# One float32 kernel of two transformer blocks: in the second block's mixers the group-norm transposes later, weight splits held back, pooled tiles in another order, and the norm factors spread one tile of k later

## The chip, the cores and the metric

The kernel runs on one core of one Trainium2 chip. The metric is the device time of one execution in microseconds (us). Engines are called PE (TensorE, matrix multiply), DVE (VectorE), ACT (ScalarE), POOL (GpSimd) and SP (the queue that issues most transfers).

## What is computed

The reference runs two transformer blocks one after the other on 256 tokens of width 1024, all in float32. Most edits lie in the second block; its core:

```python
for i in range(DEPTH):                       # DEPTH = 2
    mod = (cond @ ada_w[i] + ada_b[i]).reshape(bn, 3, 3, D_MODEL)
    h = modulate(rms_norm(x, ffn_norm[i, 0]), mod[:, 0, 0], mod[:, 0, 1])
    x = x + 0.5 * mod[:, 0, 2][:, None, :] * swiglu(h, w_gate[i, 0], w_up[i, 0], w_down[i, 0])
    h = modulate(rms_norm(x, mix_norm[i]), mod[:, 1, 0], mod[:, 1, 1])
    if i % 2 == 0:   # 31-tap conv, group_layer_norm (8 groups), silu | short gated conv
        y = conv_mixers(h, conv_w_in, ..., conv_w_out)
    else:            # means over trailing windows 2, 4, 8, 16, each a 128x128 linear | MoBA attention
        y = pool_moba_mixers(h, pm_w_in, pool_w, ..., pm_w_out)
    x = x + mod[:, 1, 2][:, None, :] * y
    h = modulate(rms_norm(x, ffn_norm[i, 1]), mod[:, 2, 0], mod[:, 2, 1])
    x = x + 0.5 * mod[:, 2, 2][:, None, :] * swiglu(h, w_gate[i, 1], w_up[i, 1], w_down[i, 1])
return rms_norm(x, final_norm)
```

The first block (four attention branches and a convolutional feed-forward, also twice) has the same shape of stages: a norm, a wide product, elementwise work, a product back to width 1024, a residual.

## The kernel before

**Layout.** Activations lie transposed: 1024 features are 8 tiles k of 128 partitions, tokens run along the free axis (272 with the 16 meta tokens in the first block, 256 in the second). An output tile is 128 features by all tokens in one PSUM bank.

**Three products for one.** Each float32 operand is split into a high and a low part (fp32r), `x = xh + xl`, and `mm3` issues three matmuls for each k: high by high, low by high, high by low. For a weight of 128x1024, `split` (line 114) writes `wh` on ACT and `split_low` (line 122) writes `wl = raw - wh` on DVE. So a weight costs PE 24 matmuls for each output tile, ACT one activation and DVE one subtraction.

**The weight stream.** All weights are one stream of chunks in order of use. `pump_dma` loads them on SP into three `raw` buffers, `prefetch` splits as far ahead as there are buffers (three of the pool `wp`, and five spare ones in the second block), `get` hands the next one to PE and asks for more. Where a split is issued on ACT and DVE is set only by where `get` or `prefetch` is called in the program: each engine works through its instructions in program order.

**Pipes and the side generator.** An output tile's eviction is a generator in steps; `advance` takes the next step of each after the next tile's matmuls, `drain` finishes all. Work of another kind (the conv taps and group norm, `gen_conv`; the attention, `gen_att`) is a side generator, of which `tick` issues a step or a few after a PE item.

**Products back into the residual.** In a mixer, `gated_gemm` is called with an order of two halves of k, (4, 0) for the conv mixer and (0, 4) for the pool mixer. A pass makes all 8 output tiles from four of the eight k, with 12 matmuls each; line 1824 adds the tile, times its gate, to the residual `h`. In the second pass `evict` also makes the square (line 1831), the raw high part `uh` (322) and the raw low part `ul` (326) of the next stage's input, and the sum of squares on POOL (1849).

**Norm after the product.** The next stage's first product, `first_gemm`, does not wait for the norm: it multiplies the raw `uh`, `ul` (gain applied, norm factor not) by four weights at once, k by k (12 matmuls a k in the second block, 9 in the first block's groups of three). After k = 1 it sums the squares over features by matmuls with ones (`tok_sums`), DVE and POOL make the factor `rs`, and after a later k `spread` copies it to all partitions by matmuls with `ident`; ACT puts the result into `pr` (line 367). Then `normed` writes the finished `uh`, `ul` for the products that follow (16 DVE operations of lines 302 and 297, 8 ACT ones of line 306, each able to overwrite a k only after PE has read it), the four output tiles are multiplied by `pr` (385), get their shift (388, 389), and `prefetch(2)` splits two weights. There are nine such products: four in the first block, five in the second.

**Group norm in the conv mixer.** `norm(j0)` runs as steps of the side generator, for channel tiles 2, 3 and then for 0, 1: mean, squares, variance, `gnr` on POOL, two transposes on PE (line 2080), `ind` matmuls that spread the factor, two products on DVE (2092), Silu on ACT (2096), the split into `oh` and `ol` (237, 238). The second pass of the product back begins with channel tile 0.

**Pooling.** `ev_u` evicts a tile u of 128 channels (line 2283), doubles its window by adds on DVE (2288: one add for window 2, four for 16), scales it and subtracts (2293, 2294). `mixed` then multiplies the four results by 128x128 weights `pw` and splits them, as input of the first pass of the product back.

Of the kernel before, what the change touches and what calls it, by code (L numbers as in the profile page):

```python
# [62 lines left out]
class Kern:  # L63
    def __init__(self, tc, a, out, w):

        self.tc, self.nc, self.a, self.out, self.w = tc, tc and tc.nc, a, out, w
        self.items = []
        self.side = deque()
        self.pipes = deque()
        self.rate = 1  # L70
        self.wait = 0
        self.spare, self.n_phase = 0, 0
        self.h = self.uh = self.ul = self.acc = self.norm = None


# [53 lines left out]
    def prefetch(self, n=99, ahead=99):  # L129

        self.pump_dma()
        while self.n_split < min(len(self.subq), self.n_used + ahead) and n:
            n -= 1
            c, _ = self.subq[self.n_split]
            out = [x for k, x in self.where.items() if self.held or k >= self.n_used]
            spare = c.spare > 0 and c.spare == self.phase and sum(out) < self.n_spare
            if not spare and len(out) - sum(out) >= NS:  # L140
                break
            while c.tile is None and self.lows:
                self.split_low()
            if c.tile is None:
                break
            self.split(self.n_split, spare)
            self.where[self.n_split] = spare
            self.n_split += 1
# [190 lines left out]
    def first_gemm(self, mk, evict, groups):  # L339

        nc = self.nc
        raw = self.norm is not None
        gain, shift, c, sums = self.norm or (None, None, slice(0, T), None)
        self.norm = None
        n, c0 = c.stop - c.start, 2 if shift else 0
        first = 0  # L350
        for g, size in enumerate(groups):
            tiles = [(w, *ms[0]) for w, ms in zip(self.get(size), mk[first:])]
            pss = [(self.gps if i < 3 else self.aps)() for i in range(size)]
            self.held = size > 1
            for k in range(KD):
                for (w, m0, m1), ps in zip(tiles, pss):
                    self.mm3(
                        ps[: m1 - m0, : n + c0], w, k, m0, m1, (self.uh, self.ul), k, c.start - c0, n + c0,
                        k == 0, k == KD - 1,
                    )  # L360
                if raw and g == 0 and k == 1:
                    r, bl = sums()
                elif raw and g == 0 and k == 2:
                    ps = self.spread(r, bl)
                    o = c.start if bl[-1][0] > 128 else 0
                    pr = self.wk.tile([128, T], F32, tag="pr", name="pr", bufs=1)[:, :n]
                    nc.scalar.activation(pr, ps[:, o : o + n], AF.Copy)
                elif k in (4, 6):
                    self.prefetch(1)
                    self.advance()  # L370
                yield
            self.held = False
            if not raw:
                for i, ps in enumerate(pss):
                    self.prefetch(1)
                    self.advance()
                    self.pipe(evict(first + i, ps))
                first += size
                continue
            if g == len(groups) - 1:  # L380
                self.normed(self.h[:, :, c], pr, gain, shift, n, (self.uh[:, :, c], self.ul[:, :, c]))
            ts = []
            for ps, (w, m0, m1) in zip(pss, tiles):
                t, m = self.w1(n), m1 - m0
                nc.vector.tensor_tensor(out=t[:m], in0=ps[:m, c0 : c0 + n], in1=pr[:m], op=MUL)
                if shift:
                    b = self.sm.tile([128, 1], F32, tag="fb", name="fb", bufs=2)
                    nc.vector.tensor_copy(b[:m], ps[:m, 0:1])
                    nc.scalar.activation(t[:m], t[:m], AF.Identity, bias=b[:m])
                ts.append(t)  # L390
            self.prefetch(2)
            while self.lows:
                self.split_low()
            for i, t in enumerate(ts):
                self.pipe(evict(first + i, t))
            first += size
            yield
# [1409 lines left out]
    def gated_gemm(self, w, kt, x, i, s, half, nxt, order=None, between=None):  # L1807
# [45 lines left out]
        for n, k0 in enumerate(order or ()):  # L1853
            end = n == len(order) - 1
            if end and between:
                between()
            for j0 in (0, 4):
                def fn(j0=j0, k0=k0, end=end):
                    if j0 == 0:
                        self.drain()  # L1860
                    xx = x()
                    for q in range(2):
                        (wt,) = self.get()
                        for m in range(2):
                            ps = self.gps()
                            for kk in range(4):
                                self.mm3(
                                    ps[:, :SEQ], wt, kk, 128 * m, 128 * m + 128, xx, k0 + kk, 0, SEQ, kk == 0, kk == 3
                                )
                            self.advance()  # L1870
                            self.pipe(evict(j0 + 2 * q + m, ps, end))
                            yield

                rows = w[k0 * 128 : k0 * 128 + 512, j0 * 128 : j0 * 128 + 512]
                self.add(fn, Chunk(rows, [[(0, 0, 256)], [(256, 0, 256)]]))
# [73 lines left out]
    def conv_mixer(self):  # L1949
# [102 lines left out]
        def norm(j0):  # L2052
# [20 lines left out]
            nc.vector.tensor_scalar(out=ms, in0=pv[:, 0:8], scalar1=1.0 / 64, scalar2=EPS, op0=MUL, op1=ADD)  # L2073
            r = self.sm.tile([128, 8], F32, tag="gn", name="gnr", bufs=2)
            nc.gpsimd.tensor_tensor(out=r, in0=ms, in1=self.mhalf[:, :8], op=ALU.pow)
            for _ in range(2 if j0 == 0 else 1):
                yield
            ps = self.aps()
            for b in range(2):
# [9 lines left out]
            for q in range(2):  # L2089
                j = j0 + q  # L2090
# [93 lines left out]
    def pool_mixer(self):  # L2184
# [123 lines left out]
        self.add(start)  # L2308
        for j in (0, 2):
            cols(1536 + 128 * j, to("v", j))  # L2310
        for j in (0, 2):
            cols(128 * j, ev_u(j))

        def mixed():
            for g in range(4):
                ps = self.gps()
                self.mm(ps[:, :SEQ], S["pw"][:, g, :], S["p", g])
                t = S["u"][:, g, 16:]
                nc.scalar.activation(
                    t, ps[:, :SEQ], AF.Identity, scale=self.v("pool_scale_2", g), bias=S["pb"][:, g : g + 1]  # L2320
                )
                self.split_act(S["oh"][:, g, :], S["ol"][:, g, :], t)
            yield

        self.add(mixed)
        self.gated_gemm(
            self.w["pm_w_out_2"][0], KD, lambda: (S["oh"], S["ol"]), 1, 1, False, (1, 2, "ffn_norm_2", 3), (0, 4),
            lambda: self.add(lambda: self.finish(G["g"])),
# [175 lines left out]
```

## Time and profile before

| | |
|---|---|
| runs | median 2204.09 us of 3 (2201.56 to 2204.61) |
| profiled execution | 2204.02 us, its span 2202.0 us |
| PE busy | 2137.4 us, 97% of the span |
| DVE busy | 1597.9 us, 73% |
| ACT busy | 1195.7 us, 54% |
| POOL busy | 173.4 us, 8% |
| granted PE clock, mean | 0.992 of full speed |
| transfers | 443.42 MB, mean 201 GB/s |

In a timeline row the first number is the start in us from the span's start, the second how long the instruction (or the merged run of `x` instructions) took; in brackets stands the engine's idle time ahead of it and whose end released it. PE's matmuls overlap: in an unbroken row of them one of 0.28 us starts every 0.12 us, so a bracket on PE leaves out some 0.16 us of the delay of the next start. In a row of waits stand the engine that waited, for whom, the us in total, how many times and the longest. In a row of the table by stretches stand the stretch, its length, each engine's busy us and instructions, the granted PE clock as a share of 2.4 GHz, the DMA share and GB/s.

### The profile page before, as it was taken

Reading aid. Unit: us, or ns where it says so; the run is one execution under the profiler, and the core shown is the slowest. Engines: PE = TensorE matmul, PEld = TensorE weight load, DVE = VectorE, ACT = ScalarE, POOL = GpSimd, SP = SyncE. Lnnn points to the kernel's source line nnn. Section 1 sums busy time; section 2 is a strip of 40 time slices with the busy share of each in tenths; the row PEclk is TensorE's granted clock in tenths of the full one; section 3 lists DMA queues with packets and bytes.
Section 4 is the critical chain, followed back from the end, with each engine's and each line's share of the span. In section 5 each row is a group of like instructions: output and inputs, shape, how many; then the busy total and the mean of one; then the engine's idle time right before and its main releaser. Section 6 shows DMA issues by size and latency. Waiting matters only on the chain. (4 is left out here: it accounts for less than half of the span.)

```text
span 2202.0 us, 42228 instructions
## 1 busy us (share of the span) xinstructions
PE 2137.4 (97%) x17234; PEld 2051.9 (93%) x17234; DVE 1597.9 (73%) x2833; ACT 1195.7 (54%) x2164; POOL 173.4 (8%) x223
## 2 busy tenths in 40 slices
PE   7999999999989999999999899999999999999998
PEld 7898989899979899898999899999999999989998
DVE  5665555888985656558989877797877877777553
ACT  4556454667456554547765644455544544476442
POOL 1320111100031101111000100001000000001000
PEclk9999999999999999999999999999999999999999
DMA  7653234454854342345559687555777687744552
GB/s 281 196 199 125 97 134 156 180 181 174 316 201 161 126 151 104 128 167 184 207 186 361 240 289 270 216 204 189 253 276 285 253 284 269 261 154 163 183 178 72
DMA packets 74322, 443.42 MB, mean 201 GB/s; under 512 B 14477, under 2 KB 15821, under 8 KB 26128
## 3 DMA queue, kind: packets, MB, share of 16 engines
q1 hardware_dynamic: 63312, 423.85, 53.7%
q0 software_dynamic: 10528, 16.79, 2.6%
q8 instruction: 135, 2.21, 0.4%
q14 instruction: 59, 0.48, 0.1%
q10 hardware_dynamic: 288, 0.07, 0.0%
HBM read 437.32 MB, written 10.01 MB: 203 GB/s over the span
## 5 line engine op out<-in xcount | busy, mean ns | idle before, releaser
L227 PE MATMUL g<-uh,wh 128*128 128x256 f32 (+2 forms) x3560 | 1028.0, 289 | 11.1 <-ACT uh L322 6.2
L227 PE MATMUL g<-ul,wh 128*128 128x256 f32 (+2 forms) x3560 | 1019.9, 286 | 10.8 <-DVE ul L326 6.3
L227 PE MATMUL g<-uh,wl 128*128 128x256 f32 (+2 forms) x3560 | 1016.6, 286 | 3.2 <-DVE wl L122 3.2
L122 DVE TENSOR_TENSOR wl<-raw,wh 128x1024 fp32r<-128x1024 f32 (+2 forms) x668 | 787.9, 1185 | 274.5 <-ACT wh L114 273.2
L114 ACT ACTIVATE wh<-raw 128x1024 fp32r<-128x1024 f32 (+2 forms) x668 | 678.3, 1020 | 348.3 <-PE g L227 313.7
L227 PEld LDWEIGHTS g<-uh,wh 128*128 128x128 f32 x3560 | 674.3, 189 | 34.1 <-issue 13.8
L227 PEld LDWEIGHTS g<-ul,wh 128*128 128x128 f32 x3560 | 673.1, 189 | 16.4 <-DVE ul L326 7.1
L227 PEld LDWEIGHTS g<-uh,wl 128*128 128x128 f32 x3560 | 675.1, 190 | 4.4 <-DVE wl L122 4.0
L227 PE MATMUL g<-gh,wh 128*128 128x256 f32 (+1 forms) x1056 | 299.2, 283 | 0.0
L227 PE MATMUL g<-gh,wl 128*128 128x256 f32 (+1 forms) x1056 | 299.2, 283 | 0.0
L227 PE MATMUL g<-gl,wh 128*128 128x256 f32 (+1 forms) x1056 | 299.0, 283 | 0.0
L227 PEld LDWEIGHTS g<-gl,wh 128*128 128x128 f32 x1056 | 201.5, 191 | 0.0
L227 PEld LDWEIGHTS g<-gh,wh 128*128 128x128 f32 x1056 | 201.3, 191 | 0.0
L227 PEld LDWEIGHTS g<-gh,wl 128*128 128x128 f32 x1056 | 201.3, 191 | 0.0
L1774 DVE CUSTOM_DVE_ANT_0 adaw<-adaw,condb,vec 128x1024 f32<-128x1024 f32 x144 | 182.4, 1279 | 0.0
L1677 DVE SCALAR_TENSOR_TENSOR y<-edge,vec,y 128x272 f32<-128x272 f32 (+1 forms) x176 | 86.4, 493 | 29.5 <-ACT y L1672 26.2
L227 PE MATMUL g<-oh,wh 128*128 128x272 f32 (+1 forms) x296 | 87.8, 297 | 0.0
L227 PE MATMUL g<-ol,wh 128*128 128x272 f32 (+1 forms) x296 | 84.8, 287 | 0.0
L227 PE MATMUL g<-oh,wl 128*128 128x272 f32 (+1 forms) x296 | 84.8, 286 | 0.0
L1920 ACT ACTIVATE sg<-g 128x256 f32<-128x256 f32 x80 | 30.5, 382 | 99.1 <-PE g L227 99.0
L1276 ACT ACTIVATE gt<-g 128x272 f32<-128x272 f32 (+1 forms) x64 | 25.1, 392 | 101.8 <-PE g L227 101.7
L1670 ACT ACTIVATE edge<-g 128x272 f32<-128x272 f32 (+1 forms) x82 | 32.3, 393 | 59.3 <-PE g L227 59.1
(384 smaller groups left out, 2311.5 us busy)
## 6 DMA issues: line engine op xcount, KB each, us to landing
raw<-in_weights_dram SPq DMA_DIRECT2D x298, 1024.0 KB, 5.0
adaw<-in_ada_t_dram SPq DMA_DIRECT2D x72, 1024.0 KB, 6.1
raw<-in_weights_dram SPq DMA_DIRECT2D x28, 768.0 KB, 5.0
skew<-scr POOLq DMA_DIRECT2D x6, 1086.0 KB, 23.0
h<-skew POOLq DMA_DIRECT2D x16, 272.0 KB, 3.7
h<-skew POOLq DMA_DIRECT2D x8, 512.0 KB, 5.2
condb<-cond SPq DMA_DIRECT2D x5, 512.0 KB, 4.7
hd<-h SPq DMA_DIRECT2D x2, 1088.0 KB, 8.9
```

The costliest lines, as they stand in the source:

```text
L114: self.nc.scalar.activation(h3[:, :, d0 : d0 + n], c.tile[:, :, c0 : c0 + n], AF.Copy)
L122: self.nc.vector.tensor_tensor(out=l3[:, :, d0 : d0 + n], in0=c.tile[:, :, c0 : c0 + n], in1=h3[:, :, d0 : d0 + n].bitcast(F32), op=SUB,)
L227: self.nc.tensor.matmul(out, lhsT, rhs, start=start, stop=stop, skip_group_check=True)
L1276: nc.scalar.activation(t[:, :rn], ps[:, :rn], AF.Tanh, scale=0.5)
L1670: nc.scalar.activation(e[:, 1 + r0 : 1 + r0 + rn], ps[:, :rn], AF.Copy)
L1677: nc.vector.scalar_tensor_tensor(out=y, in0=e[:, o : o + on], scalar=cw(i), in1=y, op0=MUL, op1=ADD)
L1774: self.nc.vector.tensor_tensor_reduce(out=t[:, i, :], in0=t[:, i, :], in1=self.condb, scale=1.0, scalar=self.v("ada_b_2", c), op0=MUL, op1 ...
L1920: nc.scalar.activation(t, ps[:, :SEQ], AF.Silu)
```

## The change

Four edits:

- `spread` is issued after k = 3 and no longer after k = 2 of a `first_gemm`; this holds for all nine of them.
- A field `cap` bounds how far `prefetch` splits. At the start of the last pass of an ordered `gated_gemm` it is set to the next 8 weights, which are the last pass's four and the next `first_gemm`'s four; it is lifted after the last k of that `first_gemm`.
- In the group norm of channel tiles 0, 1 the side generator yields four times instead of two between the POOL operation and the transposes.
- The pool mixer makes its u tiles 2, 3, 0, 1 instead of 0, 1, 2, 3, `mixed` works in that order, and it also stands, empty but for a yield, as an item after the first two.

```diff
--- before.py
+++ after.py
@@ -70,6 +70,7 @@
         self.rate = 1
         self.wait = 0
         self.spare, self.n_phase = 0, 0
+        self.cap = 1 << 30
         self.h = self.uh = self.ul = self.acc = self.norm = None
 
 
@@ -132,7 +133,7 @@
 
 
         self.pump_dma()
-        while self.n_split < min(len(self.subq), self.n_used + ahead) and n:
+        while self.n_split < min(len(self.subq), self.n_used + ahead, self.cap) and n:
             n -= 1
             c, _ = self.subq[self.n_split]
             out = [x for k, x in self.where.items() if self.held or k >= self.n_used]
@@ -360,7 +361,7 @@
                     )
                 if raw and g == 0 and k == 1:
                     r, bl = sums()
-                elif raw and g == 0 and k == 2:
+                elif raw and g == 0 and k == 3:
                     ps = self.spread(r, bl)
                     o = c.start if bl[-1][0] > 128 else 0
                     pr = self.wk.tile([128, T], F32, tag="pr", name="pr", bufs=1)[:, :n]
@@ -377,6 +378,7 @@
                     self.pipe(evict(first + i, ps))
                 first += size
                 continue
+            self.cap = 1 << 30
             if g == len(groups) - 1:
                 self.normed(self.h[:, :, c], pr, gain, shift, n, (self.uh[:, :, c], self.ul[:, :, c]))
             ts = []
@@ -1858,6 +1860,8 @@
                 def fn(j0=j0, k0=k0, end=end):
                     if j0 == 0:
                         self.drain()
+                        if end:
+                            self.cap = self.n_used + 8
                     xx = x()
                     for q in range(2):
                         (wt,) = self.get()
@@ -2073,7 +2077,7 @@
             nc.vector.tensor_scalar(out=ms, in0=pv[:, 0:8], scalar1=1.0 / 64, scalar2=EPS, op0=MUL, op1=ADD)
             r = self.sm.tile([128, 8], F32, tag="gn", name="gnr", bufs=2)
             nc.gpsimd.tensor_tensor(out=r, in0=ms, in1=self.mhalf[:, :8], op=ALU.pow)
-            for _ in range(2 if j0 == 0 else 1):
+            for _ in range(4 if j0 == 0 else 1):
                 yield
             ps = self.aps()
             for b in range(2):
@@ -2308,11 +2312,12 @@
         self.add(start)
         for j in (0, 2):
             cols(1536 + 128 * j, to("v", j))
-        for j in (0, 2):
+        for j in (2, 0):
             cols(128 * j, ev_u(j))
-
-        def mixed():
-            for g in range(4):
+            self.add(lambda j=j: mixed(j))
+
+        def mixed(j):
+            for g in (2, 3, 0, 1) if j == 0 else ():
                 ps = self.gps()
                 self.mm(ps[:, :SEQ], S["pw"][:, g, :], S["p", g])
                 t = S["u"][:, g, 16:]
@@ -2322,7 +2327,6 @@
                 self.split_act(S["oh"][:, g, :], S["ol"][:, g, :], t)
             yield
 
-        self.add(mixed)
         self.gated_gemm(
             self.w["pm_w_out_2"][0], KD, lambda: (S["oh"], S["ol"]), 1, 1, False, (1, 2, "ffn_norm_2", 3), (0, 4),
             lambda: self.add(lambda: self.finish(G["g"])),
```

**Place 1: ACT, and the next product on PE, at the end of the conv mixer.** On ACT the rows go from the split of the last of the first product's four weights to the end of that product. `wh` is a weight's high part and `raw` the chunk it comes from, `w1_...<-h_80` the square of a residual tile, `gs` a gain, `pr` the spread norm factor, `fb` a shift. Before:

```order
L114 ACTIVATE wh_17855<-raw_17652 128x1024
...
L322 ACTIVATE uh_81<-h_80,gs_17890 128x256
L114 ACTIVATE wh_17898<-raw_17720 128x1024
...
L114 ACTIVATE wh_17941<-raw_17720 128x1024
...
L114 ACTIVATE wh_18045<-raw_17802 128x1024
L367 ACTIVATE pr_18102<-a_18099 128x256
...
L389 ACTIVATE w1_18214<-w1_18214,fb_18216 128x256
L114 ACTIVATE wh_18219<-raw_17872 128x1024
```

And now:

```order
L115 ACTIVATE wh_17855<-raw_17652 128x1024
...
L323 ACTIVATE uh_81<-h_80,gs_17890 128x256
L1833 ACTIVATE w1_17914<-h_80 128x256
...
L368 ACTIVATE pr_18097<-a_18094 128x256
...
L391 ACTIVATE w1_18194<-w1_18194,fb_18196 128x256
L115 ACTIVATE wh_18199<-raw_17720 128x1024
L115 ACTIVATE wh_18202<-raw_17720 128x1024
```

On PE the rows run from the last matmul of the first product into the next one:

```order
L228 MATMUL a_18034<-uh_81,wl_17856 128x258
L228 MATMUL g_18221<-uh_81,wh_18199 128x256
L228 MATMUL g_18221<-ul_82,wh_18199 128x256
L228 MATMUL g_18221<-uh_81,wl_18200 128x256
```

The two weights of chunk 17720, the first that PE needs after the first product, were split between the squares of the last pass; now they stand behind `pr`, the eight `uh` and the four shifts. Four splits have left the stretch on ACT, and their four low parts on DVE. At the end of the pool mixer the rows read alike.

**Place 2: DVE in the first pass of the conv mixer's product back.** `h_80<-g_...` adds an output tile of the pass to the residual, `w1<-cy,vec,a` is the normed channel tile, `col` its low part. Before, from the pass's third tile on:

```order
L1824 SCALAR_TENSOR_TENSOR h_80<-g_17747,gate_17722,h_80 128x256
L1824 SCALAR_TENSOR_TENSOR h_80<-g_17765,gate_17722,h_80 128x256
L2092 SCALAR_TENSOR_TENSOR w1_17779<-cy_16625,vec_98,a_17762 128x256
L2092 SCALAR_TENSOR_TENSOR w1_17782<-cy_16625,vec_98,a_17762 128x256
L122 TENSOR_TENSOR wl_17786<-raw_17577,wh_17785 128x1024
L1824 SCALAR_TENSOR_TENSOR h_80<-g_17788,gate_17722,h_80 128x256
L238 TENSOR_TENSOR col_16632<-w1_17779,coh_16631 128x256
L238 TENSOR_TENSOR col_16632<-w1_17782,coh_16631 128x256
```

And now, from its fifth tile on:

```order
L1826 SCALAR_TENSOR_TENSOR h_80<-g_17779,gate_17722,h_80 128x256
L1826 SCALAR_TENSOR_TENSOR h_80<-g_17799,gate_17722,h_80 128x256
L2096 SCALAR_TENSOR_TENSOR w1_17813<-cy_16625,vec_98,a_17796 128x256
L2096 SCALAR_TENSOR_TENSOR w1_17816<-cy_16625,vec_98,a_17796 128x256
L123 TENSOR_TENSOR wl_17820<-raw_17652,wh_17819 128x1024
L1826 SCALAR_TENSOR_TENSOR h_80<-g_17822,gate_17722,h_80 128x256
L239 TENSOR_TENSOR col_16632<-w1_17813,coh_16631 128x256
L239 TENSOR_TENSOR col_16632<-w1_17816,coh_16631 128x256
```

The same chain stands two output tiles, 24 matmuls, later in an unchanged pass of eight tiles. On PE the two transposes and the `ind` matmuls ahead of it have moved by the same 24 matmuls.

**Place 3: DVE at the end of the pooling.** `pl` is a windowed sum, `w1` the pooled tile, `s4` attention scores with their maximum, `pol` the low parts that the product back reads. Before, from the last weight's low part on:

```order
L122 TENSOR_TENSOR wl_23272<-raw_23084,wh_23271 128x1024
L2288 TENSOR_TENSOR pl_23301<-pu_22601 128x271
L2288 TENSOR_TENSOR pl_23303<-pl_23301 128x269
L2288 TENSOR_TENSOR pl_23305<-pl_23303 128x265
L2288 TENSOR_TENSOR pl_23307<-pl_23305 128x257
L2293 TENSOR_TENSOR w1_23309<-pl_23307,inv_22603 128x256
L2294 TENSOR_TENSOR w1_23309<-w1_23309,pu_22601 128x256
L568 ISA s4_23313,mx_23314<-a_23315,al_22602 128x128
...
L575 TENSOR_SCALAR nm_23327<-mx_23314 128x4
L238 TENSOR_TENSOR pol_22606<-pu_22601,poh_22605 128x256 x4
```

And now, from the scores' maximum on:

```order
L577 TENSOR_SCALAR nm_23306<-mx_23293 128x4
L123 TENSOR_TENSOR wl_23276<-raw_23084,wh_23275 128x1024
L2292 TENSOR_TENSOR pl_23322<-pu_22601 128x271
L2292 TENSOR_TENSOR pl_23324<-pl_23322 128x269
L2297 TENSOR_TENSOR w1_23326<-pl_23324,inv_22603 128x256
L2298 TENSOR_TENSOR w1_23326<-w1_23326,pu_22601 128x256
L239 TENSOR_TENSOR pol_22606<-pu_22601,poh_22605 128x256 x4
```

Two window adds fewer lie between the last u tile and its pooled tile, and the four score operations with their maximum have moved ahead of it. On SP one of 1 MB weight loads moves behind the three loads that open the next stage.

## Rows read from the trace of the kernel before

**Rows 1.** The page, part 1: busy time by engine.
```profile
PE 2137.4 (97%) x17234; PEld 2051.9 (93%) x17234; DVE 1597.9 (73%) x2833; ACT 1195.7 (54%) x2164; POOL 173.4 (8%) x223
```
**Rows 2.** Waits of PE, whole span: total, times, longest.
```profile
PE a L227 <- POOL rs L271: 4.2, 7, 1.2
...
PE g L227 <- DVE h L1824: 3.3, 2, 2.0
PE g L227 <- DVE wl L122: 3.2, 3, 1.2
...
PE a L2080 <- POOL gnr L2075: 1.7, 1, 1.7
```
**Rows 3.** Timeline of PE, first product after the conv mixer.
```profile
1529.41 0.39 PE L227 MATMUL g<-uh,wh 128*128 128x258 f32 x1 [2.00 <-DVE h L1824]
...
1535.42 0.28 PE L227 MATMUL a<-uh,wl 128*128 128x258 f32 x1
1536.11 0.71 PE L227 MATMUL a<-ident,rs 128*128 128x128 f32 x4 [0.41 <-POOL rs L271]
...
1538.09 0.28 PE L227 MATMUL g<-uh,wh 128*128 128x258 f32 x1
...
1543.84 0.28 PE L227 MATMUL g<-uh,wh 128*128 128x256 f32 x1
```
**Rows 4.** Timeline of ACT, the same stretch.
```profile
1536.86 0.39 ACT L367 ACTIVATE pr<-a 128x256 f32<-128x256 f32 x1 [4.78 <-PE a L227]
...
1545.63 1.71 ACT L389 ACTIVATE w<-w,fb 128x256 f32<-128x256 f32 x4 [1.03 <-DVE fb L388]
1547.25 2.00 ACT L114 ACTIVATE wh<-raw 128x1024 fp32r<-128x1024 f32 x2
```
**Rows 5.** Timeline of DVE, the same stretch.
```profile
1527.74 1.23 DVE L122 TENSOR_TENSOR wl<-raw,wh 128x1024 fp32r<-128x1024 f32 x1 [0.22 <-ACT wh L114]
1528.88 0.48 DVE L1824 SCALAR_TENSOR_TENSOR h<-g,gate,h 128x256 f32<-128x256 f32 x1
...
1537.34 0.88 DVE L302 SCALAR_TENSOR_TENSOR w<-h,gs,pr 128x256 f32<-128x256 f32 x2 [1.85 <-ACT pr L367]
...
1545.04 0.42 DVE L385 TENSOR_TENSOR w<-g,pr 128x256 f32<-128x256 f32 x1
...
1548.33 2.36 DVE L122 TENSOR_TENSOR wl<-raw,wh 128x1024 fp32r<-128x1024 f32 x2 [1.59 <-ACT wh L114]
```
**Rows 6.** Timelines of PE and DVE, conv mixer's product back, first pass into second.
```profile
1507.98 0.38 PE L227 MATMUL g<-coh,wh 128*128 128x256 f32 x1
1515.20 0.28 PE L227 MATMUL g<-col,wh 128*128 128x256 f32 x1
1514.09 0.75 DVE L238 TENSOR_TENSOR col<-w,coh 128x256 fp32r<-128x256 f32 x2
```
**Rows 7.** Timelines of PE and DVE, end of the pooling.
```profile
1968.88 0.67 PE L227 MATMUL g<-w,pw 128*128 128x256 f32 x2 [1.22 <-ACT poh L237]
1970.17 0.39 PE L227 MATMUL g<-pol,wh 128*128 128x256 f32 x1 [0.50 <-DVE pol L238]
1966.45 1.37 DVE L2288 TENSOR_TENSOR pl<-pl 128x269 f32<-128x269 f32 x3
1968.31 0.42 DVE L2294 TENSOR_TENSOR w<-w,pu 128x256 f32<-128x256 f32 x1
```
**Rows 8.** Timelines of ACT and DVE, a first product of the first block.
```profile
631.27 0.38 ACT L367 ACTIVATE pr<-a 128x272 f32<-128x272 f32 x1
631.82 0.91 DVE L302 SCALAR_TENSOR_TENSOR w<-h,vec,pr 128x272 f32<-128x272 f32 x2
```
**Rows 9.** Table by stretches: engines, granted PE clock, DMA.
```profile
1485.91:1489.30 3.39, 3.39 (x23) 2.84 (x24) 2.45 (x5) 1.83 (x3) 0.00 (x0) 1.00 0.43 179
1530.20:1533.60 3.40, 3.40 (x19) 3.40 (x17) 1.23 (x3) 1.83 (x4) 0.54 (x1) 0.50 0.93 370
1970.50:1973.90 3.40, 3.40 (x17) 2.98 (x17) 2.53 (x6) 2.59 (x10) 0.00 (x0) 0.51 0.11 19
```

## Prediction

> **What bounds the kernel now.** I read the page first, then PE's waits, then the timelines around each edited place, and last the granted clock. PE is busy for 97% of the span, DVE for 73% [rows 1], and no edit adds or removes a PE instruction, so time comes only from PE's waits and from its clock. The waits by partner are few and short: 4.2 us for the norm factor `rs`, 3.3 us for residual adds, 3.2 us for low parts `wl` [rows 2]. Everything below is which of these go, which come in their place, and where PE runs at 1.2 GHz.
>
> **The norm factor spread one k later.** At the first product after the conv mixer the last matmul of k = 2 starts at 1535.42 and the `ident` matmuls at 1536.11, 0.69 us apart where neighbours are 0.12 apart: 0.57 us lost to `rs` [rows 3]. The twelve matmuls of k = 3 cover that. All five first products of the second block show this wait, of 0.39 to 0.41 us in the bracket, and the seven waits for `rs` [rows 2] are these five and one at each end of the kernel: 5 x 0.57 = **-2.85 us**. `pr` comes about 0.9 us later for it, but the finished inputs are made while PE still has four k to go, with over 1 us to spare. The four first products of the first block have no such wait to lose. At one of them `pr` ends at 631.65 and DVE's norm work starts at 631.82 [rows 8]: the nine matmuls of a k, 1.1 us, minus the time by which `pr` stood behind other work on ACT, leave some 0.4 us, and PE waits for that work right after. At two others a weight split hides it. I take **+0.7 us** for all four; the bounds are 0 and 4 x 1.1.
>
> **The splits held back, what they give.** In the first product after the conv mixer PE waits 2.00 us at 1529.41 for a residual add to free its PSUM bank [rows 3]; on DVE that add (1528.88) stands right behind a `wl` of 1.23 us (1527.74) [rows 5]. Four such pairs, a `wh` of 1.0 us on ACT (two in 2.00) [rows 4] and a `wl` of 1.2 us on DVE, leave the stretch (place 1 of the change). Without them DVE has an add of 0.48 us and a low part about as long for each output tile of 12 x 0.12 = 1.4 us, and the wait goes: 2.00 + 0.16 of overlap = **-2.15 us**, and after the pool mixer 3.3 - 2.0 [rows 2] + 0.16 = **-1.45 us**. The wait after the conv mixer is followed by 3.4 us at clock 0.50, 1.2 GHz [rows 9], which costs half of that: **-1.7 us**. POOL's sums of squares, which share no queue with the splits, stay hidden.
>
> **The splits held back, what they cost.** Before, four weights beyond the first product lay split when it ended, and the next product ran on at 1543.84 with no gap [rows 3]. Now the first two of them are queued on ACT behind `pr`, eight `uh` and four shifts, and on DVE behind 16 norm operations and the four output tiles (place 1 of the change). That work is in the trace: the first split behind it starts on ACT at 1547.25 [rows 4] and its low part on DVE at 1548.33 [rows 5], 3.4 and 4.5 us after PE finished the first product. Measured from that end E in the changed kernel: four k, 1538.09 to 1543.84 = 5.75 us, now lie behind the spread [rows 3]. The spread itself takes 1536.11 to 1538.09, minus one k of 1.44, = 0.54; so it starts at E - 6.3. `pr` starts 0.75 later, norm work 0.48 after that (1536.86, 1537.34) [rows 4, 5], at E - 5.05. Sixteen operations at 0.40 (two in 0.88) and 0.5 us for the last handover between DVE and ACT bring the output tiles to E + 1.85; the split follows 2.2 us later (1545.04 to 1547.25), its low part 1.1 after that and 1.2 us long: E + 6.3. PE would want it at its third matmul, E + 0.24. So a wait of 6.1 us, twice, once after each mixer: **+12.2 us**. After it a weight costs ACT 1.0 and DVE 1.2 us against 2.9 on PE, so it does not come again. Weight loads do not set it: three chunks, six weights, lie loaded by then, and the one load that moves on SP behind three others is for the third of these chunks.
>
> After so long a wait I expect a stretch at the lower level, as after the 2.00 us wait [rows 3, 9]: 1.7 us each, **+3.4 us**, with 0 and 6.8 as bounds. The trace has it both ways: after the wait of 1.7 us for `gnr` [rows 2], which ended at 1485.9, the clock stayed at 1.00, and 3.4 us at 0.51 follow the waits of the pooling [rows 9]. The Trainium skill (TensorE: Matmul & The Clock Gate, What's actually happening) says that the slow clock is the resting state and that activity lifts it. By that rule both long waits end at 1.2 GHz and the sum below stays; by the stretch that stayed at 1.00 it would be 3.4 us less.
>
> **Later group-norm transposes.** The one wait for `gnr` [rows 2] is that of channel tiles 2, 3, which the change leaves alone; those of tiles 0, 1 show none, so there is nothing to gain. The chain behind them ends in `col` at 1514.09 on DVE, the first half ready at about 1514.5; PE reads it at 1515.20, the second matmul of the second pass [rows 6]: 0.7 us of slack. The chain moves by 24 matmuls (place 2), and 61 starts take 1507.98 to 1515.20 = 7.22 us [rows 6], so by 2.84 us. It overshoots: 2.84 - 0.7 = **+2.2 us** of waiting at the start of the second pass. Bounds: 0, if the chain closes up, and 2.8. Behind the waiting matmul all of the pass queues on PE.
>
> **Pooled tiles in another order.** The fourth `pw` matmul waits until 1968.88 for a pooled tile that ends on DVE at 1968.73, and the product back until 1970.17 for `pol` [rows 7]; 3.4 us at clock 0.51 follow [rows 9]. Two adds fewer, at 0.46 (three in 1.37) [rows 7], bring the last pooled tile 0.9 us forward. Most of that is given back at once, since the score matmuls that ran between the last u tile and `pw` now run before that tile, which ends later by their length. More comes behind it: the four `pol` no longer stand behind scores on DVE, and the next score matmuls fill PE between `pw` and the product. I take **-1.5 us**, a little under the two brackets together, 1.22 + 0.50; the bounds are 0 and, if the clock does not fall there either, -1.7 - 1.7 = -3.4.
>
> **Sum.** -2.85 + 0.7 - 2.15 - 1.45 - 1.7 + 12.2 + 3.4 + 2.2 - 1.5 = +8.85 us. The profiled execution took 2204.02 us, the median is 2204.09: **2212.9 us**, slower by 0.4%.
>
> **Rivals.**
> *Faster: the held-back weights cost little.* If PE waited for their low parts only as it does now at first products of the first block, 1.2 us at the longest [rows 2], and no slow clock followed, the sum would be 8.85 - 15.6 + 2.4 = -4.35 us; with the `col` wait hidden too, -6.55, 2197.5 us. For it: DVE and ACT idle in the last pass. Against: each works in program order, so idle time ahead of the norm work does not help; and in the first block one split weight is left to run on. It decides at 3.4 us for each place, clock included: below that the change gains. 7%.
> *No change that shows.* No slow clock after the long waits (-3.4) and the `col` wait hidden (-2.2): +3.25, 2207.3 us. 12%.
> *Slower still.* Low stretches twice as long after the long waits (+3.4) and one after the `col` wait (+1.7): +13.95, 2218.0 us. 15%; for it speaks that PE does only two matmuls in 6 us.
> *The bound does not bind,* because buffers held the splits back already: then the waits of rows 3 stay and only -2.85 + 0.7 + 2.2 - 1.5 = -1.45 is left, 2202.6 us. The rows of place 1 speak against it. 1%.
> That leaves 65% for the forecast.
>
> **How the numbers follow.** 0.2%, about 4.4 us, is what a measurement of this kernel can tell from no change. Slower by more than that: the forecast and the slower rival, 0.80. Faster by more: the first rival with the `col` wait hidden, 0.06 of its 7%. Within: the rest of it, the second and the fourth, 0.14. The range takes the forecast with its clock bounds, the slower rival and most of the second: 2206.5 to 2219.0.
>
> **What would show it.** In the profile after: two waits of PE for `wl` of about 6 us at the first matmuls behind the first products after the mixers, nothing there for residual adds, five waits for `rs` gone, a new wait of about 2 us for `col`, no score work between the last u tile and the fourth `pw` matmul, and clock 0.50 behind the long waits. The forecast is wrong if the next product starts within 3 us of the end of the first.

## The result, and the profile after

The changed kernel takes 2214.77 us (median of 6 runs, 2213.57 to 2215.87), the kernel before beside it 2203.2 us (6 runs): a ratio of 1.0051, 95% interval 1.0038 to 1.0064, slower by 11.6 us. The forecast was 2212.9 us, slower. The profiled execution took 2215.87 us, its span 2213.9.

PE's busy time and its waits in the changed kernel (page, part 1, and the view of waits), which answer to [rows 1, 2]:

```profile
PE 2141.0 (97%) x17234; PEld 2055.8 (93%) x17234; DVE 1596.2 (72%) x2833; ACT 1197.6 (54%) x2164; POOL 167.7 (8%) x223
```
```profile
PE g L228 <- ACT wh L115: 10.1, 2, 5.0
...
PE g L228 <- DVE wl L123: 4.1, 5, 1.2
...
PE a L228 <- POOL rs L272: 2.2, 2, 1.2
PE a L1586 <- DVE s L1548: 2.1, 1, 2.1
PE a L2084 <- POOL gnr L2079: 1.7, 1, 1.7
...
PE g L228 <- DVE col L239: 1.3, 1, 1.3
```

New on top are two waits for a split weight, 10.1 us together. The residual adds (3.3 us before) are gone, and so are five of seven waits for `rs`. Busy time rose by 3.6 us with the same 17,234 matmuls, which fits the clock: its mean fell from 0.992 to 0.989 of full speed.

PE at the start of the conv mixer's second pass, and from the end of the next first product on (answers to [rows 6] and [rows 3]):

```profile
1515.82 0.28 PE L228 MATMUL g<-coh,wl 128*128 128x256 f32 x1
1516.52 0.38 PE L228 MATMUL g<-coh,wh 128*128 128x256 f32 x1 [0.42 <-ACT coh L238]
1518.20 0.38 PE L228 MATMUL g<-col,wh 128*128 128x256 f32 x1 [1.30 <-DVE col L239]
...
1542.22 0.28 PE L228 MATMUL a<-uh,wl 128*128 128x258 f32 x1
1547.52 0.58 PE L228 MATMUL g<-uh,wh 128*128 128x256 f32 x1 [5.03 <-ACT wh L115]
1547.90 0.42 PE L228 MATMUL g<-ul,wh 128*128 128x256 f32 x1
1548.78 0.58 PE L228 MATMUL g<-uh,wl 128*128 128x256 f32 x1 [0.46 <-DVE wl L123]
```

The last matmul of the first product starts at 1542.22. With no gap the next product would follow at 1542.34; it starts at 1547.52, 5.2 us later. ACT and then DVE, in that time (answers to [rows 4, 5]):

```profile
1536.77 0.39 ACT L368 ACTIVATE pr<-a 128x256 f32<-128x256 f32 x1 [5.68 <-PE a L228]
...
1544.82 1.71 ACT L391 ACTIVATE w<-w,fb 128x256 f32<-128x256 f32 x4 [1.03 <-DVE fb L390]
1546.43 1.99 ACT L115 ACTIVATE wh<-raw 128x1024 fp32r<-128x1024 f32 x2
```
```profile
1544.22 0.42 DVE L387 TENSOR_TENSOR w<-g,pr 128x256 f32<-128x256 f32 x1
...
1547.50 2.36 DVE L123 TENSOR_TENSOR wl<-raw,wh 128x1024 fp32r<-128x1024 f32 x2 [1.59 <-ACT wh L115]
```

On ACT the first `wh` starts behind the last of four shifts, its `wl` behind that: the queue that the prediction laid out. The granted clock over both long waits and behind them (table by stretches, columns as in [rows 9]; the second and fourth row begin with the first matmul behind each long wait):

```profile
1542.30:1547.50 5.20, 0.20 (x2) 0.00 (x0) 3.36 (x13) 3.69 (x8) 0.00 (x0) 0.99 0.00 0
1547.50:1554.20 6.70, 6.21 (x27) 5.92 (x28) 5.97 (x8) 4.35 (x9) 0.00 (x0) 0.50 0.45 160
2017.60:2022.80 5.20, 0.20 (x2) 0.00 (x0) 3.35 (x13) 3.70 (x8) 0.00 (x0) 0.91 0.00 0
2022.80:2028.70 5.90, 5.41 (x23) 5.12 (x24) 5.09 (x6) 5.43 (x8) 0.00 (x0) 0.50 0.43 133
```

### The profile page after: what moved, and what is told of

Same layout as the page of the kernel before. It is cut to its first block, busy times and chain, and to the rows that moved or that the text cites. A ratio compares the mean times of both kernels' runs of the same rounds, so it can differ in the third digit from the quotient of the medians.

```text
span 2213.9 us, 42237 instructions
## 1 busy us (share of the span) xinstructions
PE 2141.0 (97%) x17234; PEld 2055.8 (93%) x17234; DVE 1596.2 (72%) x2833; ACT 1197.6 (54%) x2164; POOL 167.7 (8%) x223
## 4 chain that ended last, share of the span: by engine, by line
PE 78%; issue 10%; DVE 6%; DMA 3%; ACT 2%; POOL 1%; SPq 0%; POOLq 0%; DVEq 0%; ACTq 0%
PE g L228 68%; PE a L228 7%; DVE wl L123 1%; DMA skew<-scr 1%; ACT wh L115 1%; DMA adaw<-in_ada_t_dram 1%; DVE w L303 1%; PE a L664 1%; POOL h L1632 1%; PE a L1586 0%; DVE s L570 0%; DVE ul L298 0%; PE a L703 0%; DVE adaw L1776 0%; PE a L673 0%
## 5 line engine op out<-in xcount | busy, mean ns | idle before, releaser
L228 PE MATMUL g<-uh,wh 128*128 128x256 f32 (+2 forms) x3560 | 1030.6, 289 | 18.5 <-ACT wh L115 10.1
```

The costliest lines, as they stand in the source:

```text
L228: self.nc.tensor.matmul(out, lhsT, rhs, start=start, stop=stop, skip_group_check=True)
```

## The experiments

PE runs the same matmuls in all kernels, but for the two fills, and outside the edited places in one order. So the start of the n-th matmul can be set against that of the kernel before. The table gives what each profiled execution gained (-) or lost in each stretch, in us; stretches are named by the time in the kernel before.

| kernel | to 1506 | 1506–1527, second pass starts | 1527–1543.5, first product, conv | 1543.5–1560, behind it | to 1960 | 1960–1992, pooling | 1992–2011, first product, pool | 2011–2035, behind it |
|---|---|---|---|---|---|---|---|---|
| forecast | +0.1 | +2.2 | -4.4 | +7.8 | -1.1 | -1.5 | -2.0 | +7.8 |
| the change | +0.9 | +2.1 | -4.5 | +8.8 | -0.2 | -1.6 | -2.2 | +8.4 |
| cap_alone | -1.9 | -0.3 | -4.5 | +8.0 | 0.0 | 0.0 | -2.2 | +7.2 |
| no_cap | -0.4 | +3.6 | -3.9 | 0.0 | -1.1 | -1.6 | -0.7 | 0.0 |
| split_first | +0.1 | +2.1 | -4.5 | +3.8 | -0.8 | -1.6 | -2.2 | +3.8 |
| fill | -0.8 | +2.0 | -4.4 | +12.4 | -1.1 | -1.6 | -2.2 | +12.3 |
| fill2 | +0.2 | +2.1 | -4.5 | +6.4 | -1.2 | -1.6 | -2.2 | +6.3 |
| lift_early | -0.4 | +3.6 | -4.5 | +1.8 | -1.1 | -1.6 | -2.2 | +1.8 |
| k2 | -0.4 | +2.0 | -4.5 | +7.1 | +0.1 | -1.6 | -2.2 | +7.4 |
| gn_back | +1.5 | -0.2 | -4.4 | +8.0 | -0.7 | -1.6 | -2.2 | +8.2 |
| pool_back | +0.9 | +3.5 | -4.5 | +7.7 | 0.0 | -1.5 | -2.2 | +7.7 |
| three | -3.2 | -0.3 | -4.4 | 0.0 | -1.0 | -1.6 | -2.2 | 0.0 |
| three_pool_back | -2.8 | -0.3 | -4.4 | 0.0 | -1.2 | -1.6 | -2.2 | 0.0 |
| three_no_hold | -0.3 | 0.0 | +0.9 | 0.0 | -0.9 | -1.6 | -0.6 | 0.0 |

The added matmuls of the two fills are left out of the count. The column to 1506 varies by 5 us, in the first block, mostly by where stretches at half clock fall; medians carry that too.

**The hold alone (cap_alone).** The kernel before with `cap` and nothing else:

```diff
+            if end:
+                self.cap = self.n_used + 8
```

> The kernel before with nothing but the held-back splits. Theory (the held-back weights queue behind the norm work): per mixer a wait of about 6.2 us at the next product and 3.4 us of clock behind it, less the PSUM waits of 2.15 and 1.45 us and the 1.7 us of slow clock after the first of them: 2 x 9.6 - 5.3 = +13.9 us on the kernel before, about 2217 us. The rs waits of 0.57 us and the waits at the pooling stay. Rival (the loss of the whole change comes from its other parts, the later transposes above all): within 3 us of the kernel before.

2211.15 us against 2202.02, 1.0039 (1.0025 to 1.0053): the loss is the hold's. It is 9.1 us, not 13.9. The expectation had taken 3.4 us for each slow stretch (6.8 us at half speed), but PE also waits in it (see fill2). And waits fell that it had kept:

```profile
PE g L228 <- ACT wh L115: 8.7, 2, 4.3
...
PE a L228 <- POOL rs L272: 3.4, 5, 1.2
```

Five waits for `rs` stand here against seven [rows 2]; the two behind the mixers are gone. POOL's operation for `rs` and what DVE does beside it, at the first product after the conv mixer, in the kernel before:

```profile
1534.43 1.62 POOL L271 TENSOR_TENSOR rs<-ms,mhalf 128x2 f32<-128x2 f32 x1 [3.69 <-DVE ms L269]
1534.27 1.22 DVE L122 TENSOR_TENSOR wl<-raw,wh 128x1024 fp32r<-128x1024 f32 x1
```

And in cap_alone, where no low part stands there and DVE is idle from 1528.38 to 1530.70:

```profile
1528.46 0.71 POOL L272 TENSOR_TENSOR rs<-ms,mhalf 128x2 f32<-128x2 f32 x1 [3.42 <-DVE ms L270]
```

The same operation takes 0.9 us longer beside a `wl`, more than the 0.57 us that PE loses; without the `wl` it ends 0.4 us before PE wants it (1529.58). So these two waits came from the split on DVE. The long waits are 0.7 us shorter than in the change, since `pr` comes one k earlier.

**The other three parts alone (no_cap).**

```diff
-            if end:
-                self.cap = self.n_used + 8
```

> The changed kernel without the held-back splits; its other three parts stay. Theory: no long wait for a split weight after the mixers, the waits for residual adds of 2.0 and 1.3 us are back, five rs waits stay gone: -2.85 + 0.7 + 2.2 - 1.5 = -1.45 us on the kernel before, about 2202 us. Rival (the loss comes from the other parts): about 2214 us still.

2200.10 us, 0.9995 (0.9985 to 1.0004): no change that shows, and no long wait. The rival falls. The later transposes cost 3.6 us here, as 3.4 us at half clock follow their wait:

```profile
1518.20:1521.40 3.20, 3.20 (x17) 3.20 (x17) 1.61 (x6) 1.27 (x5) 0.40 (x1) 0.50 0.46 118
```

**Splits ahead of the norm work (split_first).**

```diff
-            self.cap = 1 << 30
+            if self.cap < 1 << 30:
+                self.cap = 1 << 30
+                self.prefetch(2)
+                while self.lows:
+                    self.split_low()
```

> The changed kernel, but at the end of the first product the two held-back weights are split ahead of the norm work instead of behind it; nothing is computed differently. Theory (place in the in-order queues): the wait of 5.2 us at the next product's first matmul falls to under 1 us, and what is left is a later wait of 1 to 3 us for the output tiles, which now stand behind the splits; with the slow stretch shortened or gone, 8 to 16 us less than the changed kernel, 2199 to 2207 us. Rival (the weights' loads or free buffers set the wait, not the queue): the wait of 5.2 us stays and the norm work is late on top, no faster than the changed kernel.

2205.78 us, 1.0017 (1.0008 to 1.0026). The next product starts 0.12 us after the first, with the clock at 1.00; what is left are short waits for finished inputs behind the splits, and one of 0.64 us for a later low part:

```profile
1541.40 0.28 PE L228 MATMUL a<-uh,wl 128*128 128x258 f32 x1
1541.52 0.28 PE L228 MATMUL g<-uh,wh 128*128 128x256 f32 x1
...
1542.77 0.38 PE L228 MATMUL g<-ul,wh 128*128 128x256 f32 x1 [0.17 <-DVE ul L298]
```

The same two splits of the same loads, only in another place of the queue: the place was the cause, not loads or buffers.

**The price of the clock (fill, fill2).** Forty matmuls behind each of the two first products, before the wait:

```diff
...
+                for _ in range(40):
+                    self.mm(idle[:, :SEQ], w[0][:, 7, m0:m1], self.uh[:, 7, META:T])
```

In fill2 the last line is another:

```diff
...
+                    self.mm(idle[:, :SEQ], w[0][:, 7, m0:m1], w[0][:, 5:7, m0:m1])
```

> The changed kernel with 40 matmuls more behind each of the two first products, of operands that are at hand, into a free PSUM bank that nobody reads: about 4.7 us of work for TensorE in the wait of 5.2 us, so the waits for the weights end when they did. Theory (the slow clock behind each wait follows from TensorE standing idle, and costs 3.4 us each): the granted clock stays at 1.00 behind both waits and the time falls by 6.8 us, to about 2208 us. Rival (the slow stretches are not due to the idle time, or cost nothing because other engines set the pace there): the time stays within 1 us of the changed kernel.

2223.11 us, 1.0096 (1.0081 to 1.0111): a miss, by an edit that disturbed what it was to measure. The fills read `uh` of k = 7, and the norm's last write goes into that place. ACT, in order, stood still until they were done:

```profile
1540.74 0.51 ACT L307 ACTIVATE uh<-w,mod 128x256 fp32r<-128x256 f32 x1 [0.28 <-DVE w L303]
1545.55 0.51 ACT L307 ACTIVATE uh<-w,mod 128x256 fp32r<-128x256 f32 x1 [4.30 <-PE a L228]
1547.09 1.71 ACT L395 ACTIVATE w<-w,fb 128x256 f32<-128x256 f32 x4 [1.03 <-DVE fb L394]
1548.70 1.99 ACT L115 ACTIVATE wh<-raw 128x1024 fp32r<-128x1024 f32 x2
```

From the last `uh` to the split are 3.15 us here (1545.55 to 1548.70) and 3.15 in the change (1543.28 to 1546.43): the weights hang on the norm work.

> As the run before with 40 more matmuls behind each of the two first products, but their operands are now two pieces of a split weight that nothing rewrites in that stretch, so that no norm work has to wait for them; nobody reads their result. Theory (the slow clock follows from the idle time, and costs 3.4 us at each place): the split weights land when they do in the changed kernel, the clock stays at 1.00 behind both, and the time falls by 6.8 us against the changed kernel: 4 to 6 us above the kernel before. Rival (the stretch at half clock costs nothing by itself): 11 to 12 us above the kernel before, as the changed kernel.

2211.10 us, 1.0034 (1.0022 to 1.0045). The clock is 1.00 behind both waits:

```profile
1547.00:1554.00 7.00, 6.25 (x51) 6.04 (x52) 7.00 (x10) 6.29 (x11) 0.00 (x0) 1.00 0.47 165
...
2013.40:2020.00 6.60, 5.64 (x45) 5.23 (x44) 4.75 (x15) 4.99 (x10) 0.00 (x0) 1.00 0.00 0
```

So the idle time brings the slow stretch. The gain is 4.5 us in the table (2.4 and 2.1), under the 6.8 expected. The wait by itself is worth 6.4 and 6.3 us; in the two other kernels with the long waits and the same spread (gn_back, pool_back) the clock adds 1.3 to 1.9 us to that. The traces show why it is less than half of 6.8 us. The slow stretch begins 0.1 to 2.6 us before the long wait ends, and PE then waits for the low part as well, whatever the clock (at full speed more, 0.76 us in place of 0.46). From the first matmul on that low part, 5.5 and 4.6 us of the stretch are left in the change (1548.78 to 1554.26 the first time), 3.7 and 4.2 in gn_back, 3.0 and 3.1 in pool_back; the loss is 0.2 to 0.3 us under half of that each time.

**The hold lifted early (lift_early).**

```diff
                     r, bl = sums()
+                    if self.cap < 1 << 30:
+                        self.cap = 1 << 30
+                        self.prefetch(3)
+                        while self.lows:
+                            self.split_low()
```

> The changed kernel, but the hold on the splits ends behind k = 1 of the first product, where ACT and DVE have nothing to do before the norm factor is spread: three weights are split there. Theory (what costs is only the place behind the norm work; the gain at the residual adds is from keeping the splits out of the stretch ahead): no long wait, no half clock behind the two first products, and the residual adds still not waited for: 5 to 6 us under the kernel before. Rival (the three splits push the norm work back, which is then what the product waits for): a wait of 2 to 4 us for finished inputs at both places, within 2 us of the kernel before.

2201.03 us, 0.9989 (0.9980 to 0.9998). Long waits and slow clock behind the first products are gone, but 1.8 us stay at each, so the gain is 2.4 us by the ratio and not the 5 to 6 expected. DVE shows why:

```profile
1533.60 3.50 DVE L123 TENSOR_TENSOR wl<-raw,wh 128x1024 fp32r<-128x1024 f32 x3
1538.33 1.22 DVE L123 TENSOR_TENSOR wl<-raw,wh 128x1024 fp32r<-128x1024 f32 x1 [1.23 <-ACT wh L115]
1539.47 0.87 DVE L303 SCALAR_TENSOR_TENSOR w<-h,gs,pr 128x256 f32<-128x256 f32 x2
```

The three splits fit. The fourth, which the unbound `prefetch(1)` of k = 4 adds behind `pr`, holds the norm work back by 2.0 us: the rival's mechanism, but for the fourth split and not for the three.

**The spread back (k2).**

```diff
-                elif raw and g == 0 and k == 3:
+                elif raw and g == 0 and k == 2:
```

> The changed kernel with the norm factor spread behind k = 2 again. Theory with the new reading (the held-back weights stand behind pr, so spreading later by one k lengthens both long waits by 0.7 us): five rs waits of 0.57 us back, the two waits for the weights down from 5.0 to 4.3 us, 0.7 us less in the first block: about +0.8 us on the changed kernel. Rival (the terms of the prediction add up without touching each other): long waits of 5.0 us still, +2.2 us.

2213.37 us, 1.0042 (1.0029 to 1.0055), no slower than the change. The long waits are the 8.7 us of cap_alone, as expected, but only three of the five waits for `rs` return: those away from the mixers. So the two terms touch each other twice; the rival (adding up) falls, and of the first reading the count of five.

**The transposes back (gn_back).**

```diff
-            for _ in range(4 if j0 == 0 else 1):
+            for _ in range(2 if j0 == 0 else 1):
```

> The changed kernel with the group-norm transposes where they were. Theory (the later chain overshoots its slack): the wait of 2.1 us at the start of the conv mixer's second pass is gone and nothing takes its place: -2.1 us on the changed kernel. Rival (the inputs of the second pass are late for another reason, such as the splits of coh and col behind other work): the wait stays, no change.

2212.62 us, 1.0038 (1.0024 to 1.0052). By the times that can't be told from the change; in the trace the wait is gone and the stretch is 2.3 us shorter.

**The pooled tiles back (pool_back, three_pool_back).** The second is the same edit made on `three`, below.

```diff
-        for j in (2, 0):
+        for j in (0, 2):
...
-            for g in (2, 3, 0, 1) if j == 0 else ():
+            for g in range(4):
```

> The changed kernel with the pooled tiles in the old order. Theory: the waits ahead of the fourth pooled product and of the product back return, 1.5 us, and with them the stretch at half clock of the kernel before where it falls as it did there, 1.7 us: +1.5 to +3.2 us on the changed kernel, 13 to 15 us above the kernel before. Rival (the fewer waits of the changed kernel at the pooling come from the rest of the change): no change.

2216.30 us, 1.0065 (1.0053 to 1.0078), not told from the change by its times. In the trace the pooling takes what it takes in the new order (-1.5 and -1.6), although its two old waits are back. Only cap_alone, of the kernels run, lost the 1.5 us there. Clock of cap_alone, then of pool_back, behind those waits:

```profile
1971.70:1974.90 3.20, 3.20 (x15) 2.89 (x17) 2.61 (x6) 2.80 (x10) 0.00 (x0) 0.50 0.00 0
```
```profile
1977.80:1981.20 3.40, 3.40 (x26) 2.89 (x27) 2.83 (x7) 2.91 (x10) 0.00 (x0) 1.00 0.00 0
```

> The fastest kernel so far (three splits behind k = 1, transposes and first-block spread as before) with the pooled tiles in the old order. The traces of the run before read as if the order itself were worth nothing and only the half-clock stretch of 1.7 us at the pooling differed. Theory from that reading: from the u tiles to the first score products behind the product back the old order takes the same time within 0.3 us where the clock stays at 1.00, and 1.7 us more where a stretch at half clock falls there, so 0 to +1.7 us, 8 to 10.5 us under the kernel before. Rival (the prediction's term: the two waits cost 1.5 us whatever the clock does): +1.5 us with the clock at 1.00.

2192.81 us, 0.9967 (0.9954 to 0.9979), beside 0.9954 (0.9940 to 0.9967) for the new order. The stretch is equal within 0.1 us at clock 1.00 in both. At the same clock the order of the tiles is worth nothing; the 1.5 us are the half-clock stretch of [rows 9]. Whether the new order keeps that stretch away stays open: two of four profiles in the old order have it, none of ten in the new one.

**Three splits early, and the losing parts undone (three).**

```diff
-                elif raw and g == 0 and k == 3:
+                    if self.cap < 1 << 30:
+                        self.cap += 3
+                        self.prefetch(3)
+                        while self.lows:
+                            self.split_low()
+                elif raw and g == 0 and k == (3 if size == 4 else 2):
...
-            for _ in range(4 if j0 == 0 else 1):
+            for _ in range(2 if j0 == 0 else 1):
```

> The changed kernel with three things different: three of the held-back weights, and no fourth, are split behind k = 1 of the first product; the group-norm transposes stand where they were; the norm factor is spread behind k = 3 only where the first product has four output tiles (second block), behind k = 2 in the first block. Theory (the gains are the rs waits, the residual adds and the pooled tiles; the losses were the place of the splits and the later transposes): against the kernel before -0.6 us at each of the three first products away from the mixers' ends, -4.7 us at the conv mixer and -3.7 us at the pool mixer, 9 to 10 us in all, about 2192 us. Rival (the three splits alone already push the norm work back, as the four of the earlier run did): waits of 1.7 us for finished inputs stay at both places, about 2196 us.

2191.64 us against 2202.67, 0.9954 (0.9940 to 0.9967): faster than the kernel before by 10.1 us by the ratio, and than the change by some 21 (23 between the medians). DVE's low parts now end just ahead of the norm work, and no wait follows:

```profile
1526.99 3.49 DVE L123 TENSOR_TENSOR wl<-raw,wh 128x1024 fp32r<-128x1024 f32 x3
1530.84 0.88 DVE L303 SCALAR_TENSOR_TENSOR w<-h,gs,pr 128x256 f32<-128x256 f32 x2 [0.36 <-ACT pr L373]
```
```profile
1536.00:1540.00 4.00, 4.00 (x36) 4.00 (x35) 3.24 (x12) 2.61 (x6) 0.00 (x0) 1.00 0.00 0
```

**The same without the hold (three_no_hold).** The two lines of cap_alone taken out of `three`.

> The fastest kernel so far without holding any split back. Theory (the hold by itself is worth the waits for residual adds, with what else those cost): the waits of 2.0 and 1.3 us at the first products behind the two mixers return with 0.2 us of overlap each, and perhaps a stretch at half clock of 1.7 us behind the first: +3.6 to +5.3 us, 5 to 6.5 us under the kernel before. Rival (the splits now stand elsewhere and the residual adds get through anyway): no change.

2197.67 us against 2201.28, 0.9984 (0.9975 to 0.9993), some 6.6 us slower than `three` by the ratios. The residual adds are waited for again (3.3 us, as in [rows 2]), and 6.8 us at half clock follow in the profile (the slowest of its 11 runs), twice what followed in the kernel before:

```profile
1530.40:1537.10 6.70, 6.70 (x34) 6.70 (x32) 2.29 (x5) 1.40 (x3) 1.69 (x2) 0.50 0.92 359
```

## Why the prediction was right, point by point

- **Long waits, +12.2 forecast.** 6.4 + 6.3 = 12.7 us with the clock kept up (fill2). PE starts on the first low part at 1548.78, 6.4 us after the end of the first product; the prediction's steps gave 6.3. It waits in two parts, 5.0 us for `wh` and 0.46 for `wl`, where the sign named one wait of 6 us for `wl`. Mechanism shown by split_first, fill and lift_early: place in the in-order queues of ACT and DVE.
- **Slow clock behind them, +3.4 (bounds 0 to 6.8).** 4.5 us in the profile of the change, 2.7 and 3.5 in the two other kernels of that kind. The stretches were twice as long as in [rows 9], which the prediction had given to a rival, but cost less than half their length, as part of each passed while PE waited. That twice the length at less than half the price came near 3.4 us is in part luck.
- **What the hold gives, -2.15, -1.45 and -1.7.** 4.5 us at the first product after the conv mixer and 2.2 after the pool mixer, with one `rs` wait of 0.57 in each: the sizes hold. Undone in three_no_hold.
- **`rs`, -2.85.** All five waits went, but the prediction's cause holds for three: two go by the hold alone (cap_alone, k2), and there the later spread only lengthens the long wait, by 0.7 us. The prediction took POOL's work to be untouched, as it shares no queue with the splits; POOL's operation is slower beside one all the same (1.62 us against 0.71).
- **First block, +0.7.** Not settled. At the product named (631) the change loses nothing that lasts (0.0 us from 629 to 640). It loses 0.6 us from 1224 to 1232, at the fourth product, where PE's wait for a finished input grows from 0.35 to 0.95 us. Other kernels with k = 3 lose 0.2 to 1.0 us there, those with k = 2 from -0.1 to 0.5, but slow stretches fall there in many.
- **Later transposes, +2.2.** 2.1 us (0.58 and 1.56 between starts), gone in gn_back. The prediction's own difference, 2.84 - 0.7, is 2.1 too.
- **Pool order, -1.5.** This step failed in its cause: the amount came by luck, from the clock. The two brackets, 1.22 and 0.50 us, became 1.14 us at the same `pw` matmul and 0.29 us for `s` at 1982.46: most of the waiting had moved, not gone.
- **The rest.** The table sums to 11.7 us, the forecast to 8.85. Of the 2.9 between, 1.5 lie behind the two first products (mostly the clock), 1.0 between 1560 and 1960 and 0.7 ahead of 1506; the other places take some 0.3 back. The 1.0 holds a new wait for `mx` (0.74 us at 1946.64), the 0.7 a longer one for `s` (2.1 us against 1.0, at 1213.55). No edit touches either place, and the stretch from 1560 to 1960 varies among the other kernels too. That the sum comes near the measured time is in part luck, since terms with the wrong cause came out in the right size.

## What to carry to other kernels

Work taken out of a busy stretch goes back into in-order queues somewhere: follow it to the new place, count what stands ahead of it, and put it into idle time that lies before the next dependent chain, bounded in number. Two terms that pass through the same chain don't add up, so test them together and apart. An engine that shares no queue with the moved work can still change its pace: compare how long its operations take with that work beside them and without. A wait can bring a slow stretch or not, so look at the clock in several profiles before giving a gain to an edit.

## What the runs showed of the hardware

- 6.8 us at clock 0.50, begun 0.1 to 2.6 us before the wait ended, came with both 5.2 us waits here, and likewise with the long waits of cap_alone, fill, k2, gn_back and pool_back. With PE filled (fill2) the clock stayed at 1.00.
- After short waits it went either way. Behind the 0.58 and 1.56 us at the second pass 3.4 us at half clock followed in three kernels (no_cap, lift_early, pool_back) and none in the change, split_first, fill, fill2 and k2. After the pooling's waits in the old order, the kernel before and cap_alone slowed, pool_back and three_pool_back did not. In the new order none of the profiles shows it. What decides is open.
- POOL's operation for `rs` took 1.5 to 1.6 us at each first product of the second block with a `wl` running on DVE, and 0.7 us without. Its 128x256 adds into `acc` behave alike in the profiles of all kernels: 1.39 to 1.42 us beside a `wl`, 0.73 to 0.82 otherwise.
